# Rotary embedding: making the main sine and cosine tables in two halves and fixing VectorE's order

## The chip, the cores and the metric

The kernel runs on one core of one Trainium2 chip. The metric is the device time of one execution in microseconds; it lies some 2 us above the span that a profile shows. Executions come fast and slow; slow is one that took over 1.5% longer than the fastest of the same kernel. Times are compared fast with fast.

## The reference

```python
# x: 8 x 8 x 1024 x 64 float32; freqs: 32; positions: 1024
half = x.shape[-1] // 2
angles = np.outer(positions, freqs)
cos, sin = np.cos(angles), np.sin(angles)
x_first, x_second = x[:, :, :, :half], x[:, :, :, half:]
out_first = x_first * cos - x_second * sin
out_second = x_first * sin + x_second * cos
```

16.8 MB are read and 16.8 MB are written, whatever the kernel does in between.

## The kernel before

VectorE makes the angles in turns, takes off the whole turns, and ScalarE takes sine and cosine. The table of 64 positions a partition (`sin_c`, `cos_c`) serves 62 heads in eight groups. Two heads are read as f32 (`xf`), have a small table of their own (`sin_r`, `cos_r`), and their results are written from `of`.

```python
    def tables(pos_f, n, copies, name, pin=lambda i: i):
        turns = singles.tile([P, n, half], f32, name=f"turns{name}")
        pin(v.tensor_mul(out=turns, ...))                       # L95
        ...
        pin(v.tensor_scalar(out=whole, in0=turns, ...))         # L99
        pin(v.tensor_sub(out=turns, in0=turns, in1=whole))      # L101
        ...
        nc.scalar.activation(out=sin[:, :, 0], in_=turns, func=Act.Sin, scale=twopi)         # L105
        pin(v.tensor_scalar_mul(out=sin[:, :, 1], in0=sin[:, :, 0], scalar1=-1.0))           # L106
        nc.scalar.activation(out=whole, in_=turns, func=Act.Abs)
        nc.scalar.activation(out=cos, in_=whole..., func=Act.Sin, scale=-twopi, bias=half_pi)
```

GpSimd issues all reads of the groups (they become bf16 on the way), then waits for the first half of the last read, and only then issues the groups' writes. SyncE (SP) writes the two heads and the last 16 rows of the last group.

```python
    pool.keepalive_nop(ins=[pool.lower_ap(xts[-1][:, :run // 2])])      # the release
    for i, ((lo, n), xt) in enumerate(zip(groups, xts)):
        ...
        rotate(xt, n * chunks, ot, 0, hi, ...)                          # L151, L152, L154
        tc.keep_in_program_order(pool.dma_start(out=hbm(out, lo, n, 0, hi * d), in_=...))    # L184
        if i == 1:
            of = rotate_first()
    ...
    sp.keepalive_nop(ins=[sp.lower_ap(xts[-1][:, :run // 2])])
    for i in range(edge):
        tc.keep_in_program_order(sp.dma_start(out=hbm_head(out, i), in_=of[:, i]))           # L198
    for i, done in enumerate(ots[:-1]):
        sp.clobber_nop(...)             # L200: waits for each output's landing
    for r in range(0, tail, R):
        tc.keep_in_program_order(sp.dma_start(out=..., in_=last[:, r:r + R]...))             # L203
```

## Time and profile before

| | before |
|---|---|
| time, median of 4 | 84.35 us (84.22, 84.34, 84.36, and 87.52) |
| span | 82.1 us |
| VectorE busy | 67.6 us |
| transfers issued by GpSimd, share of the 16 engines' span | 95.0% |

The prediction below shows the lines of the page, of the stretches and of the waits. To these come the lines of the timeline that the change is about. Each has start, duration, engine, line, operation, operands and, in brackets, the idle time before it and what ended it.

```profile
7.07 0.01 DVE L88 LOAD_MASK_SELECT const<-const  x1 [2.28 <-DMA const<-in_freqs_dram]
...
11.34 2.29 DVE L101 TENSOR_TENSOR turnsc<-turnsc,wholec 128x2048 f32<-128x2048 f32 x1
...
15.61 0.69 DVE L106 TENSOR_SCALAR sinc<-sinc 128x2048 bf16<-128x2048 bf16 x1 [1.98 <-ACT sinc L105]
...
75.54 1.22 DVE L154 TENSOR_TENSOR last<-last,t 128x1024 f32<-128x1024 f32 x1
76.79 0.81 SPq L203 DMA_DIRECT2D out_dram<-last  x2
```

VectorE starts on the tables when the frequencies have landed, at 7.07. It finishes the angles at 13.63 and stands still for 1.98 us while ScalarE takes the sines. Its last addition ends at 76.76, and the last writes go out at once.

### The profile page before, as it was taken

To read this page: it belongs to the slowest core of one execution; us is meant where nothing else is said; L and a number is where in the kernel's file an instruction comes from. 1 tells how busy PE (TensorE), PEld (TensorE's weight loads), DVE (VectorE), ACT (ScalarE), POOL (GpSimd) and SP (SyncE) were. 2 spreads that over 40 slices of the span, in tenths; PEclk is the share of its full clock that TensorE was granted. 3 is DMA by queue.
4 is the path that set the end of the run, shared out by engine and by line. 5 is a ranking of instruction groups with operands and counts; after the bars stand their busy time and mean duration, and the time that the engine had idled before them with its cause. 6 is when DMAs were issued, how large, how long until landed. Compare 5 with 4: busy or idle time off the path is not lost.

```text
span 82.1 us, 157 instructions
## 1 busy us (share of the span) xinstructions
DVE 67.6 (82%) x49; ACT 9.4 (11%) x8; POOL 9.5 (12%) x22
## 2 busy tenths in 40 slices
DVE  0135996399999996999999999999999999999300
ACT  0600003999000007000000000000000000000000
POOL 4970300000000000000340020002002002002000
DMA  1999999999999999999999999999999999999992
GB/s 19 304 225 212 204 232 216 204 224 212 225 213 204 228 216 200 228 202 208 212 417 415 447 423 439 439 399 463 431 415 447 415 455 431 399 455 405 437 379 104
DMA packets 3456, 25.45 MB, mean 310 GB/s; under 512 B 560, under 2 KB 576, under 8 KB 1600
## 3 DMA queue, kind: packets, MB, share of 16 engines
q0 software_dynamic: 2384, 23.86, 95.0%
q1 hardware_dynamic: 864, 1.57, 5.6%
q10 hardware_dynamic: 208, 0.02, 0.3%
HBM read 16.80 MB, written 16.78 MB: 409 GB/s over the span
## 4 chain that ended last, share of the span: by engine, by line
DVE 78%; DMA 7%; ACT 4%; issue 4%; ACTq 1%
DVE t L151 22%; DVE ot L152 21%; DVE ot L154 19%; DMA const<-in_freqs_dram 7%; DVE turnsc L101 3%; DVE turnsc L95 3%; ACT sinc L105 2%; DVE wholec L99 2%; DVE of L168 2%; DVE of L171 1%; DVE last L154 1%; DVE last L152 1%; ACT cosr L109 1%; DVE sinc L106 1%; DVE turnsr L95 1%
## 5 line engine op out<-in xcount | busy, mean ns | idle before, releaser
L151 DVE TENSOR_TENSOR t<-xt,sinc 128x4096 bf16<-128x4096 bf16 (+3 forms) x9 | 18.3, 2046 | 0.0
L154 DVE TENSOR_TENSOR ot<-ot,t 128x4096 bf16<-128x4096 bf16 (+2 forms) x8 | 17.7, 2222 | 0.2
L152 DVE TENSOR_TENSOR ot<-xt,cosc 128x4096 bf16<-128x4096 bf16 (+2 forms) x8 | 17.6, 2216 | 0.0
L184 POOL DMA_DIRECT2D out_dram<-ot x8 | 4.2, 532 | 61.4 <-DMA xt<-in_x_dram 31.5
L82 POOL DMA_DIRECT2D xt<-in_x_dram x9 | 4.9, 573 | 3.5 <-DMA xt<-in_x_dram 2.6
L105 ACT ACTIVATE sinc<-turnsc 128x2048 bf16<-128x2048 f32 x1 | 1.9, 1909 | 10.3 <-DVE turnsc L101 10.3
L106 DVE TENSOR_SCALAR sinc<-sinc 128x2048 bf16<-128x2048 bf16 x1 | 0.7, 693 | 2.0 <-ACT sinc L105 2.0
L95 DVE TENSOR_TENSOR turnsc<-pos_f,fturn 128x2048 f32<-128x2048 f32 x1 | 2.3, 2291 | 0.0
L101 DVE TENSOR_TENSOR turnsc<-turnsc,wholec 128x2048 f32<-128x2048 f32 x1 | 2.3, 2291 | 0.0
L87 DVE LOAD_MASK_SELECT const<-const x1 | 0.0, 14 | 2.7 <-DMA const<-in_positions_dram 2.7
L109 ACT ACTIVATE cosc<-wholec,half_pi 128x2048 bf16<-128x2048 f32 x1 | 2.0, 2002 | 0.1
L88 DVE LOAD_MASK_SELECT const<-const x1 | 0.0, 14 | 2.3 <-DMA const<-in_freqs_dram 2.3
L108 ACT ACTIVATE wholec<-turnsc 128x2048 f32<-128x2048 f32 x1 | 1.9, 1893 | 0.0
L105 ACT ACTIVATE sinr<-turnsr 128x256 bf16<-128x256 f32 x1 | 0.4, 416 | 10.6 <-DVE turnsr L101 10.6
L105 ACT ACT_TABLE_LOAD x1 | 1.3, 1283 | 2.1 <-issue 2.1
L168 DVE TENSOR_TENSOR of<-x,cosr 128x1024 f32<-128x1024 bf16 x1 | 1.2, 1226 | 0.1
L99 DVE TENSOR_SCALAR wholec<-turnsc 128x2048 f32<-128x2048 f32 x1 | 1.2, 1228 | 0.0
L171 DVE TENSOR_TENSOR of<-of,t 128x1024 f32<-128x1024 f32 x1 | 1.2, 1225 | 0.0
L154 DVE TENSOR_TENSOR last<-last,t 128x1024 f32<-128x1024 f32 x1 | 1.2, 1224 | 0.0
L152 DVE TENSOR_TENSOR last<-xt,cosc 128x1024 f32<-128x1024 bf16 x1 | 1.2, 1218 | 0.0
L126 ACT CAST x<-xf 128x1024 bf16<-128x1024 f32 x1 | 1.0, 1028 | 0.0
L115 DVE CAST pos_f<-const 32x64 f32<-32x64 int32 x4 | 0.8, 211 | 0.1
(17 smaller groups left out, 4.7 us busy)
## 6 DMA issues: line engine op xcount, KB each, us to landing
out_dram<-ot POOLq DMA_DIRECT2D x6, 2048.0 KB, 11.1
xt<-in_x_dram POOLq DMA_DIRECT2D x6, 1024.0 KB, 21.8
out_dram<-ot POOLq DMA_DIRECT2D x2, 1536.0 KB, 6.3
xt<-in_x_dram POOLq DMA_DIRECT2D x2, 512.0 KB, 34.3
xt<-in_x_dram POOLq DMA_DIRECT2D x1, 768.0 KB, 6.7
xf<-in_x_dram SPq DMA_DIRECT2D x2, 256.0 KB, 2.9
out_dram<-of SPq DMA_DIRECT2D x2, 256.0 KB, 2.9
out_dram<-last SPq DMA_DIRECT2D x2, 256.0 KB, 4.0
```

Source lines behind the costliest of these rows:

```text
L82: nc.gpsimd.dma_start(out=xt[:, a:b], in_=hbm(x, lo, n, a, b))
L95: pin(v.tensor_mul(out=turns, in0=pos_f.to_broadcast([P, n, half]), in1=fturn.to_broadcast([P, n, half])))
L99: pin(v.tensor_scalar(out=whole, in0=turns, scalar1=magic, scalar2=magic, op0=Alu.add, op1=Alu.subtract))
L101: pin(v.tensor_sub(out=turns, in0=turns, in1=whole))
L105: nc.scalar.activation(out=sin[:, :, 0], in_=turns, func=Act.Sin, scale=twopi)
L109: nc.scalar.activation(out=cos, in_=whole[:, :, None, :].to_broadcast([P, n, copies, half]), func=Act.Sin, scale=-twopi, bias=half_pi)
L151: pin(v.tensor_mul(out=t.rearrange(flat4), in0=xt, in1=sin_c[:n, lo:hi].rearrange(flat4)))
L152: pin(v.tensor_mul(out=ot, in0=xt.rearrange("p (c two h) -> p c two h", two=2, h=half), in1=cos_c[:n, lo:hi].to_broadcast([n, rows, 2, hal ...
L154: pin(v.tensor_add(out=ot, in0=ot, in1=swap(t)))
L168: pin(v.tensor_mul(out=o, in0=x0, in1=w.to_broadcast(flat)))
L171: pin(v.tensor_add(out=pair, in0=pair, in1=swap(t.rearrange(rows, two=2, h=half))))
L184: tc.keep_in_program_order(pool.dma_start(out=hbm(out, lo, n, 0, hi * d), in_=ot.rearrange(flat4)))
```

## The change

VectorE is to go on with the angles of the second 32 positions while ScalarE takes the sines of the first 32. The use of the small table moves behind group 2, so that its sines lie beside other work too, and VectorE's instructions from the conversion of the positions on are pinned, that is, kept in the order of the program, as are ScalarE's for the tables. The core of the diff:

```diff
+        m = n // parts
+        cuts = [slice(i * m, i * m + m) for i in range(parts)]
+        for c in cuts:
+            pin(v.tensor_mul(out=turns[:, c], ...))
+            pin(v.tensor_scalar(out=whole[:, c], ...))
+            pin(v.tensor_sub(out=turns[:, c], ...))
+        for c in cuts:
+            pin(nc.scalar.activation(out=sin[:, c, 0], in_=turns[:, c], func=Act.Sin, scale=twopi))
+            pin(nc.scalar.activation(out=whole[:, c], in_=turns[:, c], func=Act.Abs))
+            pin(nc.scalar.activation(out=cos[:, c], ...))
 ...
-    sin_c, cos_c = tables(pos_f, C, 1, "c")
+    sin_c, cos_c = tables(pos_f, C, 1, "c", 2)
 ...
+        for a in range(0, rows, m):
+            if parts > 1:
+                negate(sin_c[:, lo + a:lo + a + m])
+            pin(v.tensor_mul(out=t[:, a:a + m]..., ...))
 ...
-        rotate(xt, n * chunks, ot, 0, hi, tc.keep_in_program_order if i > 1 else lambda ins: None)
+        rotate(xt, n * chunks, ot, 0, hi, 1 if i else 2)
 ...
         if i == 1:
-            of = rotate_first()
+            first_tables = tables_first()
+        elif i == 2:
+            of = rotate_first(*first_tables)
```

More of the change, by code (lines that the diff above doesn't have):

```diff
@@ L87, with tables @@
     v.stream_shuffle(pos_i, pos_i, [i % chunks for i in range(32)])
-    v.stream_shuffle(fr, fr, [0] * 32)
-    fturn = singles.tile([P, 1, half], f32)
-    v.tensor_scalar_mul(out=fturn[:, 0, :], in0=fr, scalar1=1.0 / twopi)
-    def tables(pos_f, n, copies, name, pin=lambda i: i):
+    pin = tc.keep_in_program_order
+    def tables(pos_f, n, copies, name, parts):
         turns = singles.tile([P, n, half], f32, name=f"turns{name}")
-        pin(v.tensor_mul(out=turns, in0=pos_f.to_broadcast([P, n, half]),
-                         in1=fturn.to_broadcast([P, n, half])))
@@ L97, in tables @@
         whole = singles.tile([P, n, half], f32, name=f"whole{name}")
-        magic = 1.5 * 2.0 ** 23
-        pin(v.tensor_scalar(out=whole, in0=turns, scalar1=magic, scalar2=magic,
-                            op0=Alu.add, op1=Alu.subtract))
-        pin(v.tensor_sub(out=turns, in0=turns, in1=whole))
         sin = singles.tile([P, n, 2, half], bf16, name=f"sin{name}")
         cos = singles.tile([P, n, copies, half], bf16, name=f"cos{name}")
-        nc.scalar.activation(out=sin[:, :, 0], in_=turns, func=Act.Sin, scale=twopi)
+        magic = 1.5 * 2.0 ** 23
@@ new lines, in tables @@
+        m = n // parts
+        cuts = [slice(i * m, i * m + m) for i in range(parts)]
+        for c in cuts:
+            shape = [P, m, half]
+            pin(v.tensor_mul(out=turns[:, c], in0=pos_f[:, c].to_broadcast(shape),
+                             in1=fturn.to_broadcast(shape)))
+            pin(v.tensor_scalar(out=whole[:, c], in0=turns[:, c], scalar1=magic, scalar2=magic,
+                                op0=Alu.add, op1=Alu.subtract))
+            pin(v.tensor_sub(out=turns[:, c], in0=turns[:, c], in1=whole[:, c]))
@@ L106, in tables, with negate @@
+        for c in cuts:
+            pin(nc.scalar.activation(out=sin[:, c, 0], in_=turns[:, c], func=Act.Sin, scale=twopi))
+            pin(nc.scalar.activation(out=whole[:, c], in_=turns[:, c], func=Act.Abs))
+            pin(nc.scalar.activation(
+                out=cos[:, c], in_=whole[:, c, None, :].to_broadcast([P, m, copies, half]),
+                func=Act.Sin, scale=-twopi, bias=half_pi))
+        return sin, cos
+    def negate(sin):
         pin(v.tensor_scalar_mul(out=sin[:, :, 1], in0=sin[:, :, 0], scalar1=-1.0))
-        nc.scalar.activation(out=whole, in_=turns, func=Act.Abs)
@@ L109, in tables @@
-        nc.scalar.activation(out=cos, in_=whole[:, :, None, :].to_broadcast([P, n, copies, half]),
-                             func=Act.Sin, scale=-twopi, bias=half_pi)
-        return sin, cos
     pos_f = singles.tile([P, C, 1], f32)
     for q in range(0, P, 32):
-        v.tensor_copy(out=pos_f[q:q + 32],
-                      in_=pos_i.rearrange("p (c w) -> p c w", w=words)[:, :, :1])
-    sin_c, cos_c = tables(pos_f, C, 1, "c")
+        pin(v.tensor_copy(out=pos_f[q:q + 32],
+                          in_=pos_i.rearrange("p (c w) -> p c w", w=words)[:, :, :1]))
@@ L120 @@
+    pin(v.stream_shuffle(fr, fr, [0] * 32))
+    fturn = singles.tile([P, 1, half], f32)
+    pin(v.tensor_scalar_mul(out=fturn[:, 0, :], in0=fr, scalar1=1.0 / twopi))
+    sin_c, cos_c = tables(pos_f, C, 1, "c", 2)
     pos_r = singles.tile([P, R, words], i32)
@@ L132, in swap, with rotate @@
                        ap=[part, rows, [-half, 2], cols])
-    def rotate(xt, n):
-        flat = "p c two h -> p (c two h)"
-        ot = opool.tile([P, C, 2, half], bf16, name="ot")[:n]
-        t = tpool.tile([P, C, 2, half], bf16, name="t")[:n]
-        v.tensor_mul(out=t.rearrange(flat), in0=xt, in1=sin_c[:n].rearrange(flat))
-        v.tensor_mul(out=ot, in0=xt.rearrange("p (c two h) -> p c two h", two=2, h=half),
-                     in1=cos_c[:n].to_broadcast([n, C, 2, half]))
-        v.tensor_add(out=ot, in0=ot, in1=swap(t))
-        return ot
     flat4 = "p c two h -> p (c two h)"
-    def rotate(xt, n, ot, lo, hi, pin):
+    def rotate(xt, n, ot, lo, hi, parts=1):
         rows = hi - lo
@@ L150, in rotate @@
         t = tpool.tile([P, C, 2, half], bf16, name="t")[:n, :rows]
-        pin(v.tensor_mul(out=t.rearrange(flat4), in0=xt, in1=sin_c[:n, lo:hi].rearrange(flat4)))
+        m = rows // parts
+        for a in range(0, rows, m):
+            if parts > 1:
+                negate(sin_c[:, lo + a:lo + a + m])
+            pin(v.tensor_mul(out=t[:, a:a + m].rearrange(flat4), in0=xt[:, a * d:(a + m) * d],
+                             in1=sin_c[:n, lo + a:lo + a + m].rearrange(flat4)))
         pin(v.tensor_mul(out=ot, in0=xt.rearrange("p (c two h) -> p c two h", two=2, h=half),
@@ L154, in rotate, with tables_first, rotate_first @@
         pin(v.tensor_add(out=ot, in0=ot, in1=swap(t)))
-    def rotate_first():
-        pin = tc.keep_in_program_order
+    def tables_first():
         pos_rf = singles.tile([P, R, 1], f32)
         pin(v.tensor_copy(out=pos_rf, in_=pos_r[:, :, :1]))
-        sin_r, cos_r = tables(pos_rf, R, 2, "r", pin)
+        return tables(pos_rf, R, 2, "r", 1)
+    def rotate_first(sin_r, cos_r):
+        negate(sin_r)
         flat = [P, edge, R * d]
@@ L186 @@
         if i == 1:
-            of = rotate_first()
+            first_tables = tables_first()
+        elif i == 2:
+            of = rotate_first(*first_tables)
     last = singles.tile([P, tail, 2, half], f32)
-    rotate(xts[-1], P, last, C - tail, C, tc.keep_in_program_order)
+    rotate(xts[-1], P, last, C - tail, C)
     sp = nc.sync
```

## The prediction

> **What bounds the kernel now.** I read the page first, then the chain of waits, then the stretches, then the issuing queue's own waits, because they contradict each other. The chain names VectorE (DVE):
>
> ```profile
> DVE 67.6 (82%) x49; ACT 9.4 (11%) x8; POOL 9.5 (12%) x22
> ...
> DVE 78%; DMA 7%; ACT 4%; issue 4%; ACTq 1%
> ```
>
> On that alone a wait taken from VectorE would be worth its full length. But the slices and the queues show another full resource. The second line shows GB/s doubling at slice 21, near 41 us:
>
> ```profile
> DMA  1999999999999999999999999999999999999992
> GB/s 19 304 225 212 204 232 216 204 224 212 225 213 204 228 216 200 228 202 208 212 417 415 447 423 439 439 399 463 431 415 447 415 455 431 399 455 405 437 379 104
> ...
> q0 software_dynamic: 2384, 23.86, 95.0%
> ...
> HBM read 16.80 MB, written 16.78 MB: 409 GB/s over the span
> ```
>
> The doubling isn't a speed-up. Half of x's 16.8 MB is counted on the way in, since nearly all of it lands as bf16: 8.4 + 16.78 MB, and 0.26 MB more for the two heads that land as f32, is 25.44, the page's 25.45 MB. So the transfers move some 430 GB/s of memory bytes in both halves, and are never idle. The stretches (us, busy times, granted clock, DMA share, GB/s) say it best, with the last two after VectorE has stopped:
>
> ```profile
> 4.00:40.00 36.00, 30.67 (x29) 8.09 (x7) 2.27 (x6) 1.00 1.04 214
> 44.00:76.00 32.00, 31.79 (x17) 0.00 (x0) 2.65 (x5) 1.00 1.06 430
> 76.80:79.00 2.20, 0.00 (x0) 0.00 (x0) 0.00 (x0) 1.00 1.09 436
> 79.00:81.00 2.00, 0.00 (x0) 0.00 (x0) 0.00 (x0) 1.00 0.76 281
> ```
>
> The reads fill the transfers until 40, the writes from then on, and for 2.2 us after the last VectorE instruction they are as full as ever: they work off a backlog. The backlog also shows in the time of an output from issue to landing (min, median, max): one of 2.1 MB needs 4.9 us at 430 GB/s, and the median takes twice that.
>
> ```profile
> DMA to landing us min/median/max: 5.8/10.1/14.8
> ```
>
> No output is issued before about 40, however early VectorE has it: GpSimd, which issues them, is held until the first half of the last read has landed. Two groups had been ready long before:
>
> ```profile
> POOL out_dram L184 <- DMA xt<-in_x_dram: 31.5, 1, 31.5
> POOL out_dram L184 <- DVE ot L154: 30.0, 6, 6.2
> ```
>
> So **the bound is the transfers**, with VectorE a close second: its group takes 6.73 us (41.72 to 48.45 in the chain) against 4.9 us of writing, and it eats up the lead of three groups just before the end. At the very end one wait is VectorE's, in the queue of SyncE (SP), which issues the last two small writes:
>
> ```profile
> SPq L200 <- DMA out_dram<-ot: 33.3, 7, 4.8
> ...
> SPq L203 <- DVE last L154: 0.5, 1, 0.5
> ```
>
> That queue first waits for seven outputs to land, one after another, and only then, for 0.5 us, for VectorE's last addition. Half a microsecond is what a faster VectorE can win there.
>
> **What the Trainium skill says.** (1) "DMA: Bandwidth & Descriptors", "Where 436 GB/s comes from": the ports of SBUF give 435 GB/s, whoever issues. The trace agrees: 430 and 436 in the stretches. An estimate from it: 33.58 MB / 435 GB/s = 77.2 us, which with the 4 us before the transfers are full is 81, where they in fact end. (2) "VectorE: DVE Perf Modes", "The perf-mode tier table": a tensor-tensor operation of 2048 f32 takes 2293 ns, of bf16 1224, a tensor-scalar 1227 in f32 and 693 in bf16. The trace has 2291 for L95, 1228 for L99, 693 for L106. (3) "ScalarE: Activation LUTs", "What ACT_TABLE_LOAD costs": 0.833 ns an element and a fixed part. The trace: 1909 ns at 2048 and 416 at 256 elements, so 0.833. (4) "SBUF — State Buffer", "SBUF: two separate sides": GpSimd, which writes the descriptors of its transfers, is locked out while VectorE runs in a two-port mode. I use it for a rival below.
>
> **The change part by part.** All times are from the rows by form and the timeline of before.
>
> Part 1, order at the start: the fourth conversion (0.22 us with its gap) now stands ahead of the wait for the frequencies, so the first big multiplication starts at 7.53 instead of 7.75. -0.22.
>
> Part 2, halves: 128x2048 becomes twice 128x1024. A f32 tensor-tensor operation of 1024 takes 1.22 (the row of the last addition, L154), so four are 4.9; the tensor-scalar, between 1228 ns at 2048 and 294 at 256, is 0.69 at 1024, twice 1.39; with six gaps of 0.025, 6.44 instead of 5.89. +0.55, so the angles are finished at 13.97 instead of 13.64.
>
> Part 3, the wait: in before VectorE stands still while ScalarE takes 2048 sines (2.0 us in the row of L106). Now the first half's angles are done near 10.75, and ScalarE's sine of 1024 (1.06), its absolute value (1.04) and cosine (1.15) run from 10.77 to about 14.0 beside VectorE's second half. VectorE negates half one at once. Half two's sine ends about 15.05, its cosine about 17.24. VectorE wants that sine at 15.68 and that cosine at 17.37, so it waits for neither, though for the cosine the margin is only 0.1. -1.95. The split negation and split product of group 0 cost two more fixed parts: 2 x 0.427 against 0.693, 2 x 1.218 against 2.286, with two gaps +0.37.
>
> Up to group 0's first product: -0.22 + 0.55 - 1.95 + 0.37 = -1.25.
>
> Part 4: the small tables (L95 to L101, 1.3 us) are made after group 1, but their use comes after group 2, so ScalarE's small sine and cosine lie beside group 2's 6.7 us. The 0.5 us wait before L106 and the 0.1 before L168 go: -0.58.
>
> Part 5, pinning of groups 0 and 1: by the order of instructions, group 0 is now finished before group 1 starts. Both are still done (21.9 and 28.6) long before 40. Worth nothing.
>
> Sum on VectorE: about **-1.8 us**, so its last addition ends near 75.0 instead of 76.76. No byte less is moved, and neither the start of the reads nor the release of the writes at 40 depends on VectorE. What is left on the path to the end: the last two writes. With VectorE done at 75.0, the issuing queue meets the wait ahead of it, the landing of the seventh output at about 76.3 (0.5 before 76.79), which the transfers set. So these writes are issued **0.5 us sooner**, not 1.8, and mix with the tail of the eighth output. The stretch 79 to 81 has a share of 0.76 only, so there is room: at full share its 2 us would be 1.5. I take 0.35 us of the end. 84.35 - 0.35 = **84.0**.
>
> One small cost: the two f32 heads are finished after group 2, near 40.13 instead of 34.99, so that their writes, which went out at 40.01 the moment the read was in, may go 0.1 us later. They fill the change from reading to writing, so up to 0.1 us of transfer can be lost.
>
> **Rivals.**
> A. VectorE is the bound, as the chain of waits says. Then all of 1.8 us comes through: 82.6, 2.1% faster. For it: 78% of the chain, and its 99% busy from 44 to 76. Against it: the transfers' 436 GB/s after VectorE has ended, and outputs that take twice their transfer time to land. 5%.
> B. The end is set wholly by bytes, and even the 0.5 us at the last issue is worth nothing, as the small writes start behind the eighth output anyway: 84.35. For it: those writes took 4.0 us to land, against 2.9 for the same size at 40. This is the neighbour of my own case; I give the two together 90%.
> C. Something new gets in the way: GpSimd's last read issue (8.28 to 8.81, then a memset) now lies beside a two-port tensor-scalar (8.78 to 9.47, formerly from 10.08), and descriptors come late; or the heads' writes come later than I think, and the transfers stand idle near 42; or the late cosine makes VectorE wait. Against it: some 30 us of reads are already queued at 8.3, and VectorE has 1.8 us in hand. 84.7 to 85.
>
> **Range and chances.** The range covers the two likely cases, 84.0 and 84.35, with the 0.3% by which executions scatter and a share of C: 83.5 to 84.7. Faster by over 2% needs 82.67, which not even the whole gain on VectorE gives with any certainty: 0.04. Slower by over 2% needs 1.7 us of new idle transfers: 0.02. Same: 0.94. The one execution of 87.52 I take for a disturbed one, since the two others agree within 0.02.
>
> **What would show it right or wrong.** In the changed profile: the angles done at about 14, no idle time of 2.0 before the negation, VectorE's last addition ending near 75.0; the DMA row still all nines, q0's share still near 95%, the read-to-write change still at slice 21. In the issuing queue the 0.5 us wait for VectorE's last addition is gone, and the last writes are issued near 76.3. The span is 81.6 to 82.1. I am wrong if the last writes go out near 75, if the span shrinks by over 1.5 us, or if the transfers show a slice of less than 9 tenths around 42 that was not there before.

## The result, and the profile after

| | before | after |
|---|---|---|
| time, median of 4 | 84.35 us | 84.84 us |
| the fast executions | 84.22, 84.34, 84.36 | 84.83, 84.83, 84.85 |
| profiled span | 82.1 us | 82.9 us |

The ratio of the fast executions was 1.0063, with a 95% interval from 1.004 to 1.0086: the same within 2%, but 0.14 us above the predicted range, and with the wrong sign. Ratios are the mean time of one kernel's fast runs over that of the other's of the same rounds, so they are not quite the ratio of the medians quoted.

First VectorE, in the timeline after. L124, L107, L118, L160 and L213 answer to L88, L101, L106, L154 and L203; L158 is the product with the cosine.

```profile
7.76 0.01 DVE L124 LOAD_MASK_SELECT const<-const  x1 [2.64 <-DMA const<-in_freqs_dram]
...
13.34 1.23 DVE L107 TENSOR_TENSOR turnsc<-turnsc,wholec 128x1024 f32<-128x1024 f32 x1
...
14.48 0.42 DVE L118 TENSOR_SCALAR sinc<-sinc 128x1024 bf16<-128x1024 bf16 x1
...
16.08 0.42 DVE L118 TENSOR_SCALAR sinc<-sinc 128x1024 bf16<-128x1024 bf16 x1
...
17.83 2.29 DVE L158 TENSOR_TENSOR ot<-xt,cosc 96x4096 bf16<-96x4096 bf16 x1
...
74.32 1.22 DVE L160 TENSOR_TENSOR last<-last,t 128x1024 f32<-128x1024 f32 x1
77.11 0.81 SPq L213 DMA_DIRECT2D out_dram<-last  x2
```

The wait of 1.98 us is gone: no bracket stands behind either negation. The last addition ends at 75.54, 1.22 us sooner, although the frequencies happened to land 0.69 us later in this execution (7.76 against 7.07). Without that, by the sum, the gain is 1.91 us. But the last writes went out at 77.11, later than before. The page shows the transfers as full as ever in the rest of the span:

```profile
DVE 68.3 (82%) x54; ACT 9.9 (12%) x11; POOL 9.4 (11%) x22
...
DMA  3999999999999999999999999999999999999990
GB/s 16 305 234 210 217 221 194 233 210 218 216 199 229 214 214 225 194 212 216 210 413 395 414 459 438 427 435 411 459 419 427 435 419 459 411 427 421 439 358 32
...
q0 software_dynamic: 2384, 23.86, 94.1%
q1 hardware_dynamic: 864, 1.57, 9.4%
...
HBM read 16.80 MB, written 16.78 MB: 405 GB/s over the span
...
DVE 71%; ACT 8%; DMA 7%; issue 4%; ACTq 1%
```

VectorE's share of the chain fell from 78% to 71% and nothing was won by it. The new line here is q1, SyncE's transfers, whose packets took 9.4% of the engines' span, 5.6% before, for the same bytes. The stretches after:

```profile
4.00:40.00 36.00, 32.64 (x34) 8.57 (x10) 2.27 (x6) 1.00 1.03 214
44.00:76.00 32.00, 31.34 (x17) 0.00 (x0) 2.66 (x5) 1.00 1.15 429
76.80:79.00 2.20, 0.00 (x0) 0.00 (x0) 0.00 (x0) 1.00 1.05 419
79.00:81.00 2.00, 0.00 (x0) 0.00 (x0) 0.00 (x0) 1.00 0.89 331
```

Rates are near those of before, with VectorE idle for longer at the end. An output's time from issue to landing grew, as outputs are made sooner and wait longer in the queue:

```profile
DMA to landing us min/median/max: 7.0/11.5/15.9
```

The waits of GpSimd, and of SyncE's queue, after:

```profile
POOL out_dram L192 <- DVE of L179: 31.8, 1, 31.8
POOL out_dram L192 <- DVE ot L160: 28.5, 5, 6.2
```

```profile
SPq L210 <- DMA out_dram<-ot: 33.7, 7, 5.3
...
SPq L208 <- DVE of L179: 0.3, 1, 0.3
```

GpSimd's long wait is still that for the read. The profile names the heads' last addition because it ended last before it, but the instruction order has no such wait in it for these outputs. SyncE's 0.5 us wait for VectorE at the end is gone, as predicted, but a wait of 0.3 us for the heads (L179) has come. Their writes went out at 40.52, not 40.01. The view of the heads' tile gives their landing, before and after:

```profile
DMA to landing us min/median/max: 2.8/2.9/3.0
```

```profile
DMA to landing us min/median/max: 2.6/7.2/11.8
```

The first head's write landed in 2.6 us, the second's in 11.8. The packet records of the trace show what happened to it: in before, all 256 packets of 2 KB had started by the time that 16 packets of the bulk writes had; after, 128 of them started later than that and were dealt between the bulk's 16 KB packets. The Trainium skill says as much in "DMA: Bandwidth & Descriptors", "Queues, rings and completion order": each engine of the transfers goes round between the queues that have work for it, packet by packet.

Adding up the bytes of these records (a packet's bytes spread evenly over its time, reads that become bf16 counted at their f32 size), both kernels had moved 16.97 MB at 42 us. At 48 after had moved 19.40 MB against 19.53, and at 79 still 32.78 against 32.92. That is 0.14 MB, or 0.32 us at 430 GB/s, lost between 42 and 48 and never recovered. The last packet ended 0.76 us later; the two profiled executions, 84.83 and 84.02 us, lie 0.81 apart, more than the medians do. The rest goes with unevenness: the last 16 bulk packets (one for each of the 16 engines, if they finish evenly; the records don't name the engine) ended within 0.40 us of each other before, within 0.86 after. So the first theory was: **the change makes the heads late, their packets are dealt between the bulk, and that costs the half microsecond.** The rivals: the halves themselves or GpSimd's back-to-back issues cost it (called theory 2 in the expectations), or nothing in the program does.

### The profile page after: what moved, and what is told of

It reads as the page before. It is cut to its first block, busy times and chain, and to the rows that moved or that the text cites. A ratio compares the mean times of both kernels' runs of the same rounds, so it can differ in the third digit from the quotient of the medians.

```text
span 82.9 us, 165 instructions
## 1 busy us (share of the span) xinstructions
DVE 68.3 (82%) x54; ACT 9.9 (12%) x11; POOL 9.4 (11%) x22
## 4 chain that ended last, share of the span: by engine, by line
DVE 71%; ACT 8%; DMA 7%; issue 4%; ACTq 1%
DVE ot L158 21%; DVE t L156 19%; DVE ot L160 19%; DMA const<-in_freqs_dram 7%; ACT cosc L112 3%; ACT sinc L109 2%; ACT wholec L111 2%; DVE turnsc L107 1%; DVE turnsc L103 1%; DVE last L160 1%; DVE of L179 1%; DVE last L158 1%; DVE of L176 1%; DVE wholec L105 1%; DVE t L176 1%
## 5 line engine op out<-in xcount | busy, mean ns | idle before, releaser
L160 DVE TENSOR_TENSOR ot<-ot,t 128x4096 bf16<-128x4096 bf16 (+2 forms) x8 | 17.8, 2225 | 0.3
L158 DVE TENSOR_TENSOR ot<-xt,cosc 128x4096 bf16<-128x4096 bf16 (+2 forms) x8 | 17.7, 2218 | 0.1
L109 ACT ACTIVATE sinc<-turnsc 128x1024 bf16<-128x1024 f32 x2 | 2.1, 1048 | 8.1 <-DVE turnsc L107 8.1
L107 DVE TENSOR_TENSOR turnsc<-turnsc,wholec 128x1024 f32<-128x1024 f32 x2 | 2.5, 1225 | 0.1
L103 DVE TENSOR_TENSOR turnsc<-pos_f,fturn 128x1024 f32<-128x1024 f32 x2 | 2.4, 1221 | 0.0
L112 ACT ACTIVATE cosc<-wholec,half_pi 128x1024 bf16<-128x1024 f32 x2 | 2.3, 1148 | 0.1
L124 DVE LOAD_MASK_SELECT const<-const x1 | 0.0, 14 | 2.6 <-DMA const<-in_freqs_dram 2.6
L111 ACT ACTIVATE wholec<-turnsc 128x1024 f32<-128x1024 f32 x2 | 2.1, 1040 | 0.0
L109 ACT ACTIVATE sinr<-turnsr 128x256 bf16<-128x256 f32 x1 | 0.4, 417 | 11.8 <-DVE turnsr L107 11.8
L105 DVE TENSOR_SCALAR wholec<-turnsc 128x1024 f32<-128x1024 f32 x2 | 1.4, 694 | 0.1
L179 DVE TENSOR_TENSOR of<-of,t 128x1024 f32<-128x1024 f32 x1 | 1.2, 1224 | 0.0
L160 DVE TENSOR_TENSOR last<-last,t 128x1024 f32<-128x1024 f32 x1 | 1.2, 1224 | 0.0
L158 DVE TENSOR_TENSOR last<-xt,cosc 128x1024 f32<-128x1024 bf16 x1 | 1.2, 1218 | 0.0
```

The lines of the kernel that those rows point to most:

```text
L103: pin(v.tensor_mul(out=turns[:, c], in0=pos_f[:, c].to_broadcast(shape), in1=fturn.to_broadcast(shape)))
L105: pin(v.tensor_scalar(out=whole[:, c], in0=turns[:, c], scalar1=magic, scalar2=magic, op0=Alu.add, op1=Alu.subtract))
L107: pin(v.tensor_sub(out=turns[:, c], in0=turns[:, c], in1=whole[:, c]))
L109: pin(nc.scalar.activation(out=sin[:, c, 0], in_=turns[:, c], func=Act.Sin, scale=twopi))
L111: pin(nc.scalar.activation(out=whole[:, c], in_=turns[:, c], func=Act.Abs))
L112: pin(nc.scalar.activation(out=cos[:, c], in_=whole[:, c, None, :].to_broadcast([P, m, copies, half]), func=Act.Sin, scale=-twopi, bias=ha ...
```

## The experiments

Sixteen runs followed on four chips, four in a job, each job with 11 executions of the kernel before on its chip. (The texts speak of a second chip's scatter where they mean the first job below.)

### The heads' writes: four ways (job 1)

`a1_heads_early`, the changed kernel with the heads used before group 2 again:

```diff
-            first_tables = tables_first()
-        elif i == 2:
-            of = rotate_first(*first_tables)
+            of = rotate_first(*tables_first())
```

> The changed kernel with one thing undone: the two f32 heads are rotated before group 2 again (as in the kernel before), the halves and the pinning stay. Theory 1 (the heads' writes go out 0.5 us later, miss the gap between reads and bulk writes, and their small packets are then dealt between the bulk packets): heads done near 33.5, their two writes landing in about 3 us each, no lag of the bytes after 44 us, time 84.0 to 84.35, ratio to before 0.996 to 1.000. Theory 2 (the halves, or the three bulk writes issued back to back, or late frequencies cost the time): stays at 84.8, ratio 1.006.

`a3_before_heads_late`, the kernel before with that part of the change alone:

```diff
         if i == 1:
-            of = rotate_first()
+            first_tables = rotate_first()            # now returns its tables
+        elif i == 2:
+            of = rotate_first_use(*first_tables)     # the products and the addition
```

> The kernel before with one part of the change alone: the heads are rotated after group 2, whole tables, ScalarE wait as before. VectorE is then done with the heads near 41.7, later than in the changed kernel. Theory 1: both heads' writes now go between the bulk packets (256 packets of 2 KB, in the changed kernel some 123), so at least as slow as the changed kernel, 84.8 to 85.3, ratio 1.005 to 1.011. Theory 2: 84.35, ratio 1.000.

`a4_heads_pool`, the changed kernel with the heads' writes in the bulk queue:

```diff
             of = rotate_first(*first_tables)
+            for j in range(edge):
+                tc.keep_in_program_order(pool.dma_start(out=hbm_head(out, j), in_=of[:, j]))
 ...
-    for i in range(edge):
-        tc.keep_in_program_order(sp.dma_start(out=hbm_head(out, i), in_=of[:, i]))
```

> The changed kernel with the heads' two writes issued by GpSimd, behind group 2's write and in the same queue as the bulk, so that their packets can't be dealt between bulk packets. If dealing them between is what costs (theory 1): no lag but that of the small packets themselves, 84.2 to 84.5, ratio 0.998 to 1.002. If any write of the heads that doesn't fill the gap between reads and writes costs the same: 84.8, ratio 1.006.

`a5_heads_later`, the changed kernel with the heads held until group 0's output has landed:

```diff
+    sp.clobber_nop(outs=[sp.lower_ap(ots[0])])
     for i in range(edge):
         tc.keep_in_program_order(sp.dma_start(out=hbm_head(out, i), in_=of[:, i]))
```

> The changed kernel with the heads' writes held on purpose until group 0's write has landed (near 47 us), so that all 256 of their packets are dealt between bulk packets. Theory 1, dose: the changed kernel lost 0.32 us in bytes with some 123 packets so dealt, so about 0.65 here, and the time rises by 0.2 to 0.5 to 85.0 to 85.3, ratio 1.008 to 1.012. Theory 2: no dependence, 84.8.

| | lowest | median of all | ratio, fast runs | 95% interval | heads' landing, min/max |
|---|---|---|---|---|---|
| kernel before | 84.05 | 84.42 | | | |
| a1_heads_early | 84.21 | 85.78 | 0.9964 | 0.9873 to 1.0055 | 2.8/3.1 |
| a3_before_heads_late | 84.34 | 84.69 | 0.9996 | 0.9932 to 1.0059 | 12.9/20.2 |
| a4_heads_pool | 84.20 | 84.42 | 0.9969 | 0.9914 to 1.0023 | in the bulk queue |
| a5_heads_later | 84.35 | 84.61 | 1.0011 | 0.9945 to 1.0076 | 13.1/20.4 |

The first and third fit theory 1, though a1 has only two fast executions, and they fit as well that nothing is lost. The second and fourth don't fit it: with **all** 256 packets dealt between the bulk, the times are not 85 and more, but those of the kernel before. The dose is there in the bytes of a5's profile, if smaller than expected (0.55 us behind at 79, of which some 0.3 were lost by 44, before its heads were issued: with no packets of the heads there to fill the change from reads to writes, the engines were busy for 0.56 of the half microsecond from 41.5, by the packet records), but not in the time. All intervals hold 1. The kernel before scattered over more here than in the first comparison, 84.05 to 85.23 without its two slowest executions.

### Is VectorE the bound, and is its gain real? (job 2)

`b0_after_again` is the changed kernel, unedited. `b1_no_add` is the kernel before without group 3's addition, `b2_before_less` and `b3_after_less` are the two kernels without group 3's write. The last three give wrong results.

> The changed kernel once more, unedited, on another chip and with more rounds, since the second chip's runs of the kernel before scattered over 84.05 to 85.2. If the loss of 0.5 us belongs to the program: 84.7 to 84.9, ratio 1.004 to 1.008. If it was this chip's or that day's: 84.2 to 84.4, ratio 0.997 to 1.002.

```diff
-        pin(v.tensor_add(out=ot, in0=ot, in1=swap(t)))
+        if add:                                      # False for group 3
+            pin(v.tensor_add(out=ot, in0=ot, in1=swap(t)))
```

> The kernel before without group 3's addition, so 2.3 us less for VectorE and as many bytes (a wrong result on purpose). If the transfers are the bound: VectorE done near 74.5, time 84.0 to 84.4, ratio 0.996 to 1.000. If VectorE is the bound (rival A): 82.1, ratio 0.973.

```diff
-        tc.keep_in_program_order(pool.dma_start(out=hbm(out, lo, n, 0, hi * d),
-                                                in_=ot.rearrange(flat4)))
+        if i != 3:
+            tc.keep_in_program_order(pool.dma_start(out=hbm(out, lo, n, 0, hi * d),
+                                                    in_=ot.rearrange(flat4)))
```

> The kernel before without the write of group 3, so 2.1 MB or 4.9 us less to move and all of VectorE's work (a wrong result on purpose). If the transfers are the bound, the time falls until VectorE becomes it: the last addition still ends at 76.8, the last writes then take some 2.9 instead of 4.0, so 83.1 to 83.4, ratio 0.985 to 0.989. If VectorE is the bound already (rival A): 84.35, ratio 1.000.

> The changed kernel without the write of group 3, the same cut. With the transfers out of the way the 1.2 us that VectorE gained by the trace (75.54 against 76.76) should show in the time, against the kernel before with the same cut: 81.9 to 82.2, ratio to the uncut kernel before 0.971 to 0.975. If the gain on VectorE isn't real or something else holds the end, it's no faster than the other cut kernel.

| | lowest | median of all | ratio to before, fast runs | 95% interval |
|---|---|---|---|---|
| kernel before | 84.26 | 85.36 | | |
| b0_after_again | 84.23 | 84.74 | 0.9998 | 0.9936 to 1.0061 |
| b1_no_add: 2.3 us less VectorE | 84.24 | 86.16 | 1.0011 | 0.9899 to 1.0122 |
| b2_before_less: 2.1 MB less written | 83.20 | 84.06 | 0.9893 | 0.981 to 0.9976 |
| b3_after_less: the same cut, changed kernel | 81.52 | 82.40 | 0.9704 | 0.9616 to 0.9791 |

2.3 us less on VectorE win nothing; rival A's 0.973 lies outside the interval, though that rests on two fast executions (84.24 and 85.31). Fewer bytes do win. And once the bytes are out of the way the two kernels part: the mean of the fast executions is 82.24 (four) against 83.77 (three), so 1.5 us or 1.8% for the changed one, with a 95% interval of some 0.5 to 2.6 us worked out from these seven. Timelines and SyncE's waits of the two cut kernels, b2 first:

```profile
76.15 1.22 DVE L154 TENSOR_TENSOR last<-last,t 128x1024 f32<-128x1024 f32 x1
77.40 0.81 SPq L204 DMA_DIRECT2D out_dram<-last  x2
...
SPq L204 <- DVE last L154: 1.3, 1, 1.3
```

```profile
74.48 1.23 DVE L160 TENSOR_TENSOR last<-last,t 128x1024 f32<-128x1024 f32 x1
75.74 0.81 SPq L214 DMA_DIRECT2D out_dram<-last  x2
...
SPq L214 <- DVE last L160: 1.3, 1, 1.3
```

In both, the last writes wait 1.3 us for VectorE's last addition, and the 1.66 us between their ends (77.37 and 75.71) is what the times of these two profiled executions show (84.07 and 82.43). (Both missed their expected times by 0.2 us and more; b2's VectorE ended at 77.37 instead of 76.76, its frequencies having taken 6.1 us to land instead of 5.5.) So VectorE's gain is real, and in the uncut kernel it is hidden behind the transfers.

### Releasing the writes sooner, and a candidate (job 3)

`c3_after_third` is the changed kernel, unedited. `c2_gate_early` is the changed kernel with an earlier release; `c1_pool_early` adds to that the edits of a1 and a4, its heads' writes standing between those of group 1 and group 2. `c4_last_free` is c1 with the last writes no longer behind the landings.

> The changed kernel a third time, to settle whether its loss of 0.5 us is the program's. If it is: ratio to before 1.004 to 1.008. If it hangs on where the release of the writes falls in an execution, which varies in both kernels: 0.996 to 1.004, and the heads' write is dealt between the bulk in some profiles of both kernels.

```diff
-    pool.keepalive_nop(ins=[pool.lower_ap(xts[-1][:, :run // 2])])
+    pool.keepalive_nop(ins=[pool.lower_ap(xts[-2])])
```

> The changed kernel with the bulk writes released one read earlier (when the last but one read has landed, near 37, not the first half of the last): they then stand in the queue behind the last read, so no engine of the transfers can run dry at the changeover. If idle and skew at the changeover make up the scatter of executions: time 84.2 to 84.6 with a narrower spread, although all of the heads' packets are now dealt between the bulk. If the release isn't it: spread as before.

> A candidate that should beat both: the changed kernel with the heads rotated before group 2, their writes issued by GpSimd in the bulk queue, and the early release. No packet of the heads is dealt between bulk packets and there is no gap at the changeover. By the bytes: 33.58 MB at 430 to 435 GB/s from 3.8 us ends near 81, so 83.9 to 84.2, ratio 0.992 to 0.997. If dealing and gap aren't what costs: 84.35 or more, ratio 1.000.

```diff
-    for i, done in enumerate(ots[:-1]):
-        sp.clobber_nop(...)
     for r in range(0, tail, R):
         ...                                          # the last writes
+    for i, done in enumerate(ots[:-1]):
+        sp.clobber_nop(...)
```

> The candidate before with the last two writes issued as soon as VectorE is done (near 75.5), no longer behind the landing of the seventh output. They then lie within the eighth output's transfer, so the tail with its share of 0.76 goes: up to 0.4 us less, 83.6 to 84.0, ratio 0.989 to 0.995. If small packets dealt between bulk cost as much as the tail: equal to the candidate.

| | lowest | median of all | ratio, fast runs | 95% interval |
|---|---|---|---|---|
| kernel before | 84.24 | 84.48 | | |
| c3_after_third | 84.56 | 85.16 | 1.0036 | 0.9982 to 1.009 |
| c2_gate_early | 85.02 | 85.25 | 1.0076 | 1.0036 to 1.0116 |
| c1_pool_early | 84.93 | 85.04 | 1.0062 | 1.0021 to 1.0102 |
| c4_last_free | 84.83 | 85.49 | 1.0087 | 1.002 to 1.0153 |

The candidate failed. In c1 and c2 the scatter was narrower (84.93 to 85.47 and 85.02 to 85.44 in six executions each), in c4, which has the early release too, it wasn't (84.83 to 86.25). All three lie above the kernel before. Against c3, the kernel that it edits, c2 is 0.34 us slower, plus or minus 0.58, so that the early release alone isn't shown to cost time. By the packet records each of the three lies some 0.3 us of bytes behind by 42 us, where reads and writes meet. c2 has no idle gap there: its engines are as full from 41 to 42 (DMA share 1.05) but move 372 GB/s, where the kernel before moved 418. (a5, without an early release, is as far behind at 42, with its gap.) c2's last 16 bulk packets end within 1.06 us instead of 0.40. Why it is so wasn't tried further and stays open.

c4 answers the question of the tail. The landing of the last two writes, from the view of their tile: before, a1, and c4.

```profile
DMA to landing us min/median/max: 3.9/4.0/4.0
```

```profile
DMA to landing us min/median/max: 4.4/4.5/4.5
```

```profile
DMA to landing us min/median/max: 5.7/5.8/5.9
```

These were issued from 76.79, 76.44 and 76.27 on. The 0.35 us by which a1 issued them sooner came back as 0.5 us of longer landing, and in c4 0.52 us came back as 1.8 us. The last packets of before and a1 ended at 80.86 and 80.92. (c4 also has the early release, so its longer landing can't be put down to the sooner issue alone; c1, which has the release but not the sooner issue, took 4.3 us.)

### The changed kernel once more, with a control (job 4)

`d1_after_fourth` is the changed kernel, `d2_heads_early_again` is a1, `d3_heads_pool_again` is a4, and `d4_before_control` is the kernel before, run as though it were an experiment.

> The changed kernel, unedited. If dealing the heads' packets costs its 0.3 us and happens in this program in nearly every undisturbed execution: ratio 1.002 to 1.006, lowest time above 84.4, and a profile with some 128 packets of the heads dealt. If it is scatter: 0.998 to 1.002.

> The changed kernel with the heads rotated before group 2. If dealing is the cause: ratio 0.996 to 1.001, below the changed kernel's by 0.003 or more, lowest time near 84.1. If it is scatter: as the changed kernel.

> The changed kernel with the heads' writes in the bulk queue behind group 2, with the release where it was. If dealing is the cause: ratio 0.996 to 1.001, and, since no race between two queues is left, a spread as narrow as in its first job (84.20 to 84.46 unprofiled). If it is scatter: as the changed kernel.

> The kernel before as its own control: ratio 1.000, and the distance from 1.000 is what the method finds where nothing differs. Differences of the others below it aren't claimed.

| | lowest | median of all | ratio, fast runs | 95% interval |
|---|---|---|---|---|
| kernel before | 84.06 | 84.94 | | |
| d1_after_fourth | 84.31 | 84.89 | 0.9998 | 0.9925 to 1.0071 |
| d2_heads_early_again | 83.97 | 86.91 | none: five of six slow | |
| d3_heads_pool_again | 84.17 | 84.66 | 1.0015 | 0.9939 to 1.009 |
| d4_before_control | 84.20 | 85.62 | 1.002 | 0.9919 to 1.0122 |

The control shows the loss without the change. Its profiled execution took 85.33 us, and this is the view of its heads' tile:

```profile
L198 SPq DMA_DIRECT2D out_dram<-of x2: 348/598/849, 40.4 to 40.8; - x2
...
DMA to landing us min/median/max: 2.8/5.2/7.6
```

VectorE had these heads ready at 34.75. Still 130 of their packets were dealt between the bulk, and by the packet records this execution of the **kernel before** was at 19.40 MB at 48 us and at 32.78 at 79: the same 0.32 us behind as the changed kernel. From 43 to 46, in the view of stretches, the transfers moved 393 GB/s here and 386 in the changed kernel's profile, against 432 in the first profile of the kernel before. Its last 16 bulk packets ended within 1.42 us and its last packet at 82.16. So what the first comparison showed as a difference of two programs is a difference that two executions of one program have as well. Of the four profiles of the changed kernel three have a head's landing of 7 us or more (b0's has not), and of the four profiles with the kernel before's order in place (before, b1, b2, d4) three as well.

Pooled over all jobs, the changed kernel's 22 executions go from 84.23 to 87.96 with a median of 84.89, the kernel before's 54 (with the control) from 84.05 to 87.52 with a median of 84.91.

The dealing may still be what makes an execution slower, whatever the program: among the fast profiled executions that keep all bytes and the late release, the three without it took 84.02 to 84.21 us (before, a1, and d3 with the heads in the bulk queue), the four with it 84.60 to 85.33 (after, c3, d4, a5). That is a correlation in seven executions and not shown as a cause; a3 and a5, where all of it is dealt, reached 84.34 and 84.35. The views show one more thing: where about half of the packets were dealt, the issue of the second head's write took 0.65 to 0.90 us in SyncE's queue (0.85 in the control above), and 0.42 to 0.45 in before, b0, b1, a1 and d2, where fewer than ten packets were.

Left open: what decides in an execution whether the heads' packets are dealt, and why the heads-early kernel was slow in nine of twelve executions, which may be its order or chance. a4, the heads in the bulk queue, had the lowest ratio that rested on more than a few fast runs (0.9969) but 1.0015 when repeated, so no version here is shown to beat either kernel.

## Why the prediction was right or wrong

- **The bound.** Right. b1 and the two cut kernels show it from both sides: less VectorE wins nothing, fewer bytes win time, and the DMA row stays full. One reading of the prediction is wider than its lines: 430 and 436 GB/s are measured in the writes, while during the reads only 214 GB/s land, so that the figure for the ports agrees for the writes; for the reads it is the bytes at their f32 size that come to some 430. The section cited for the ports also says that for transfers between HBM and SBUF the side of HBM binds, at some 358 GB/s; the 430 and 436 measured here lie above that.
- **Parts 1 to 4, the sum on VectorE of -1.8 us.** Right: 1.22 in the profile, 1.91 once the frequencies' later landing (0.69) is taken off. The angles ended at 14.57, so 13.88 without that delay, against 13.97. The two halved operations took 1221 to 1225 and 694 ns, as interpolated. The cosine's margin of 0.1 was in fact a wait of 0.06.
- **Part 5.** As predicted, nothing of it shows.
- **Rival A.** Rightly at 5%: refuted by b1. Its 1.8 us appear when the bytes are cut (1.5 us between b3 and b2).
- **"What is left on the path to the end: ... issued 0.5 us sooner ... I take 0.35 us of the end."** This step failed. In the changed kernel's profile the seventh output landed at about 77.1, not at 76.3, and the last writes went out at 77.11; in c3's at 77.34. They wait for the transfers, whose bytes the change doesn't touch. Where they did go out sooner (a1, c4), they landed no sooner. The share of 0.76 between 79 and 81 was read as room, but an earlier issue didn't turn it into time. Rival B, with 0 and not 0.35, is what the repeats fit.
- **Rival C.** Its 84.7 to 85 met the first comparison's 84.84 by luck, as the repeats show. Of its forms, GpSimd's last read issue (8.20 to 8.73) had ended before the two-port operation began (9.49), as the frequencies were late, so this execution doesn't test the lock on GpSimd that the fourth citation states. None of the prediction's own three signs of being wrong came: the last writes near 75, a span shorter by 1.5 us, or a slice under 9 tenths near 42.
- **"One small cost: ... up to 0.1 us."** The direction was right for that execution, partly by luck: the heads were ready at 40.49, but without the late frequencies it would be 39.80, before the 40.01 at which the heads' writes went out in before. The prediction's 40.13 doesn't follow from its own sum either, which gives 41.72 - 1.83 = 39.89. The size was wrong: 0.32 us of bytes. But the control has the same loss without late heads, so the change is not shown to cause it. My theory 1 as the program's loss fell with a3, a5 and the control.
- **The range: "with the 0.3% by which executions scatter".** This is the step that put the time outside. I took the scatter from three executions, two of which agreed within 0.02 us, although the profiled execution that I read, 84.02, lay 0.33 below the 84.35 that I started from. Among executions called fast the same kernel went from 84.05 to 85.23 in job 1, and its own control ran at 85.33. Repeated, the ratios of the changed kernel were 0.9998, 1.0036 and 0.9998, so "same" holds. No single one of these intervals excludes both -0.35 and +0.5 us; the mean of the three differences (-0.01, +0.22 and -0.01 us, fast executions) is 0.07, plus or minus 0.27, and does.

So where did the expected gain go? It went to idle time: VectorE ends 1.2 us sooner and the transfers end when they did. The gain was off the path from the start; what the prediction added at the end of the path, and the scatter that it allowed for, were wrong.

## What to carry to other kernels

Before taking a wait off the engine that the chain names, look whether the transfers are still full after that engine has ended: here 436 GB/s with VectorE idle said that hardly any VectorE gain could show. To prove such a hidden gain, cut bytes from both kernels alike and see whether they part. And run the unchanged kernel against itself before believing half a percent: an interval from three executions each excluded 1, and three repeats in other jobs didn't confirm it.

## What the Trainium skill lacked or had wrong

- "DMA: Bandwidth & Descriptors", "Queues, rings and completion order", says that an engine goes round between queues, but not what a small write pays for it: 256 KB that landed in 2.9 us ahead of the bulk took 7.0 to 21.2 us when dealt between bulk packets.
- The same page has no word on when to release writes behind reads in one queue: the three kernels that release them one read sooner (c1, c2, c4) were slower than the kernel before by 0.6 to 0.9%, and the one of them with no other edit moved 372 GB/s instead of 418 from 41 to 42 us, with full engines; why is open.
- The same page, "Latency and other measured facts", gives some 0.6 us to the first byte for transfers issued by SyncE or ScalarE. For the frequencies, a load of 2 KB issued by ScalarE beside the bulk reads, the first packet started 3.9 us after the issue (before and after) and the landing took 5.3 to 7.1 us in these profiles, and it moved the start of VectorE's tables.
- "Perfetto Trace Analysis", "Identifying the Most-Contended Engine", rightly warns to judge transfers by the bytes rather than by occupancy. It lacks the simple test used here: the rate in the stretch after the other engine's last instruction (436 GB/s from 76.8 to 79).
- No page tells how far executions of one program scatter: 84.05 to 85.23 us, slow ones left out, for the kernel before in job 1, and 84.02 to 84.36 in the first comparison with its profiled execution.
